# A hybrid attention block on one core: first loads in order of need, first low parts on GpSimd, and attention keys padded with zeros to 128 rows

## The chip, the core and the metric

The kernel runs on one core of one Trainium2 chip. The metric is the device time of one execution in microseconds (us); the number for the kernel before is the median of three runs. One more execution was taken by the hardware profiler, and every row shown here is from it.

Engine names: PE is TensorE (matrix multiply), PEld its weight loads, DVE is VectorE, ACT is ScalarE, POOL is GpSimd. SP only issues transfers. L394 is line 394 of the kernel.

## What is computed

One decoder layer, cut to what matters (512 tokens, width 1024, everything in float32):

```
h     = rms_norm(x, norm1_g)
proj  = h @ w_in                       # attention q, k, v; GLA q, k, v, r, low rank gate; branch gates
q, k  = rms_norm(q, gq), rms_norm(k, gk)      # 3 groups x 8 heads of 64
A     = softmax attention of 3 groups (window, dilation) = (128,1), (512,4), (2048,16),
        merged per head slot by the softmax denominators
B     = gated linear attention, 4 heads, rms_norm * silu(r)
x     = x + (sigmoid(gA) * (A @ w_attn) + sigmoid(gB) * (B @ w_gla)) @ w_out
x     = x + relu(rms_norm(x, norm2_g) @ w_up)^2 @ w_down
```

## The kernel before

**Products in three parts.** Every large matrix product is done with both operands split into a high part (type fp32r) and a low part: `split` (L105) makes a weight's high part `whi` by a copy on ACT (L78) and its low part `wlo = raw - whi` on DVE (L81), 128x1024 elements at a time. A product is then three matmuls of 128x512 for each 128x128 block: high with high, high with low, low with high (L155 to L157 in `mm_tok`, L136 to L138 in `mm_cols`). Below, such a matmul is called a projection matmul.

**Start.** x comes in four tiles of 128 tokens, 0.5 MB each; the first 512 columns of w_in in two loads of 1 MB (`raws`); norm1_g is broadcast to all 128 partitions by one 0.5 MB transfer, `g1b` (L203). The loads are issued from two queues: x0 and the weights from SP, `g1b` and the other x tiles from ACT (L202 to L208). For each tile `norm_in` squares x on ACT with a sum, `rsqrt` alternates DVE and ACT, L218 multiplies by the factor and by `g1b` on DVE; `trans_in` turns the tile on PE (8 transposes, L224), ACT copies the turned tile as high part `hTh`, DVE makes the low part `hTl`. Between two tiles stands one `split` of 2 of the 8 blocks of rows of the first weights. ACT and DVE keep the order in which this is written (`manual_schedule`, L232); PE's and POOL's order comes from the scheduler. POOL meanwhile makes the masks (affine selects at L262 to L288) and issues small column loads (L255, L96). Its order is fixed when the program is built, and no engine overtakes within its own order.

The first `mm_tok` uses the four splits of the start: 96 projection matmuls, over 4 token tiles and 8 row blocks. The second one follows; after 48 of its matmuls come the first turns of `qkv` (L328, 4 transposes each).

**Attention.** `qkv` (L307) makes for each group q and k, normalises them per head, and turns them so that a tile holds two heads on its 128 partitions: head 2p in rows 0 to 63, head 2p+1 in rows 64 to 127. The learned gains go in as a scale `gqk` when k is copied from PSUM to SBUF on ACT (L329). `attend` (L343) does for four tiles of 128 queries and for pairs of heads: scores on PE (L379 for the first group, L394 for the other two), masked row maximum on DVE (L357), exponential on ACT, four transposes of the probabilities on PE (L363), a copy on DVE (L365), product with v on PE (L369). A score matmul reads 64 rows of q and 64 rows of k: its array form is 64x128. Projection matmuls of the next products stand between these steps in PE's order. A float32 matmul that is not a transpose leaves two MATMUL records in the trace: 32 score matmuls at L379 are 64 records, 64 at L394 are 128.

PSUM has 5 banks for products (`mm`) and 3 for everything else (`aux`). Big SBUF tiles live in numbered slots that are used again.

Of the kernel before, what the change touches and what calls it, by code (L numbers as in the profile page):

```python
# [16 lines left out]
P = 128  # L17
# [24 lines left out]
def kernel(ctx: ExitStack, tc: tile.TileContext, x, norm1_g, w_in, q_g, k_g,  # L42
# [153 lines left out]
    g1b = slot(8, [P, D], "g1b")  # L196
    raws = [slot(10 + j, [P, 4, 512], f"raw{j}") for j in range(2)]

    def load_in(j):
        nc.sync.dma_start(raws[j], w_in[4 * j * P:4 * (j + 1) * P, 0:512].rearrange("(k p) n -> p k n", p=P))  # L200

    nc.sync.dma_start(xs[0][:, 0], x[0:P])  # L202
    nc.scalar.dma_start(g1b, bass.AP(tensor=norm1_g.tensor, offset=norm1_g.offset, ap=[[0, P], [1, D]]))  # L203
    load_in(0)
    nc.scalar.dma_start(xs[0][:, 1], x[P:2 * P])
    load_in(1)
    for i in (2, 3):
        nc.scalar.dma_start(xs[1][:, i - 2], x[i * P:(i + 1) * P])  # L208

    def norm_in(i):  # L210
        xi, hi_ = xs[i // 2][:, i % 2], hs[i // 2][:, i % 2]
        ss = sm(1, "ss")
        act(hi_, xi, AF.Square, accum_out=ss)
        r = sm(1, "r")
        rsqrt(r, ss, D, 1)
        for j in range(2):
            cs = slice(j * 512, (j + 1) * 512)
            nc.vector.scalar_tensor_tensor(hi_[:, cs], xi[:, cs], r, g1b[:, cs], op0=OP.mult, op1=OP.mult)  # L218

    def trans_in(i):  # L220
        bs = [aux() for _ in range(2)]
        hi_ = hs[i // 2][:, i % 2]
        for k in range(KB):
            nc.tensor.transpose(bs[k // 4][:, k % 4 * P:(k % 4 + 1) * P], hi_[:, k * P:(k + 1) * P], ident)  # L224
        for j in range(2):
            bv = bs[j].rearrange("p (k t) -> p k t", k=4)
            dh = hT.hi[j][:, :, i * P:(i + 1) * P]
            act(dh, bv, AF.Copy)
            last = tt(hT.lo[j][:, :, i * P:(i + 1) * P], bv, dh.bitcast(F32), OP.subtract)
        return last  # L230

    with tc.manual_schedule(engines={mybir.EngineType.Activation, mybir.EngineType.DVE}):  # L232
        def split_in():
            j = len(first)
            first.append(split(raws[j // 2][:, j % 2 * 2:j % 2 * 2 + 2], [2, 512]))

        norm_in(0)
# [7 lines left out]
        trans_in(2)  # L245
        norm_in(3)
        split_in()
        last = trans_in(3)


    with tc.issue_after(last.ins):
        qk_cols = consts.tile([P, 2], F32, name="qk_cols")
        for j, g in enumerate((q_g, k_g)):
            for hf in range(2):
# [3 lines left out]
                                       op0=OP.mult, op1=OP.mult)  # L258

# [47 lines left out]
    def qkv(g, lhs, sq, sk, sv):  # L307
        res = []
        for kind, s in ((0, sq), (1, sk)):
            banks = mm_tok(w_in, kind * 1536 + g * 512, lhs)  # L310
            dst = slot(s, [P, 4, S], f"a{kind}{g}")
            for i in range(NT):
# [12 lines left out]
                def turn(s2=s2, d=dst[:, :, i * P:(i + 1) * P], kw={"scale": gqk} if kind else {}):  # L325
# [6 lines left out]
            res.append(dst)  # L332
# [54 lines left out]
    q2T, k2T, v2 = qkv(1, hT.perm, 4, 5, 6)  # L387
    q3T, k3T, v3 = qkv(2, hT.perm, 7, 8, 13)
    o23 = slot(9, [P, NT, 512], "o23")

    def scores23(dst, pr, hf, i):
        r = slice(hf * E, hf * E + E)
# [505 lines left out]
```

## Time and profile before

| what | value |
|---|---|
| median of three runs | 1044.24 us (1043.93 to 1044.44) |
| the profiled execution's own time | 1045.75 us |
| its span, first to last instruction | 1043.8 us |
| PE busy | 1019.7 us, 98% of the span |
| DVE, ACT, POOL busy | 661.7, 501.6, 74.5 us |
| mean granted TensorE clock | 0.998 of full speed |

How to read it: the profiled execution took 1.5 us more than the median and its span leaves out some 2 us around the program. Busy time of matmuls overlaps, because the next one starts before the last has ended: for PE one reads the distance between starts, not the duration. In a row of the timeline the first number is the start, the second the time from the first start to the last end of the instructions merged in it, the number behind x their count, and in brackets stands the idle time before with what ended it.

### The profile page before, as it was taken

The numbers are of one execution on the slowest core, as the hardware profiler recorded it, in microseconds if no ns is written. First come the engines' busy times: TensorE is split into PE (matmuls) and PEld (weight loads), VectorE is DVE, ScalarE is ACT, GpSimd is POOL, SyncE is SP. The second block draws the span as 40 slices with busy tenths as digits, with TensorE's granted clock in tenths as the row PEclk, the third lists the DMA queues.
The fourth block names the chain that finished last, engine by engine and source line by source line (L and its number), as shares of the span: only waits on it lengthen the run. The fifth ranks groups of instructions, "written<-read, shape, count | busy, mean of one in ns | idle before, by whom it ended". The sixth has DMA issues, their size and how long they took to land.

```text
span 1043.8 us, 12458 instructions
## 1 busy us (share of the span) xinstructions
PE 1019.7 (98%) x4768; PEld 857.3 (82%) x4768; DVE 661.7 (63%) x1113; ACT 501.6 (48%) x835; POOL 74.5 (7%) x112
## 2 busy tenths in 40 slices
PE   4999999999999999999999999999999999999998
PEld 3888889999888788788888888877888888888886
DVE  4654354535444632889866747985885795796695
ACT  4434343424433423667645973365553553553552
POOL 9110001001000000010002200000000000000000
PEclk9999999999999999999999999999999999999999
DMA  7222102223201312312122234263133224225102
GB/s 262 72 91 81 41 1 81 81 89 101 94 1 41 93 61 81 121 41 81 41 82 76 86 130 162 72 206 114 43 123 120 80 82 160 82 81 161 41 1 80
DMA packets 63898, 92.36 MB, mean 88 GB/s; under 512 B 3232, under 2 KB 37024, under 8 KB 63840
## 3 DMA queue, kind: packets, MB, share of 16 engines
q1 hardware_dynamic: 61056, 86.02, 25.0%
q10 hardware_dynamic: 2368, 5.28, 1.4%
q8 instruction: 37, 0.61, 0.2%
q0 software_dynamic: 416, 0.28, 0.2%
q14 instruction: 21, 0.17, 0.0%
HBM read 89.44 MB, written 2.13 MB: 88 GB/s over the span
## 4 chain that ended last, share of the span: by engine, by line
PE 94%; DVE 3%; ACT 2%; DMA 1%; issue 0%; SPq 0%; DVEq 0%
PE mm L136 11%; PE mm L137 11%; PE mm L138 11%; PE mm L155 10%; PE mm L157 10%; PE mm L156 9%; PE mm L730 4%; PE mm L729 4%; PE mm L731 4%; PE aux L369 3%; PE aux L731 2%; PE aux L730 2%; PE aux L729 2%; PE aux L394 2%; PE aux L363 2%; PE aux L379 2%
## 5 line engine op out<-in xcount | busy, mean ns | idle before, releaser
L81 DVE TENSOR_TENSOR wlo<-wraw,whi 128x1024 fp32r<-128x1024 f32 x127 | 155.5, 1225 | 147.0 <-ACT whi L78 145.1
L78 ACT ACTIVATE whi<-wraw 128x1024 fp32r<-128x1024 f32 x127 | 134.3, 1057 | 186.1 <-PE mm L157 83.8
L155 PE MATMUL mm<-whi,hTh 128*128 128x512 f32 x416 | 171.4, 412 | 4.9 <-ACT hTh L78 4.8
L157 PE MATMUL mm<-whi,hTl 128*128 128x512 f32 x416 | 167.4, 403 | 0.0
L156 PE MATMUL mm<-wlo,hTh 128*128 128x512 f32 x416 | 166.4, 400 | 0.1
L155 PEld LDWEIGHTS mm<-whi,hTh 128*128 128x128 f32 x416 | 102.3, 246 | 15.6 <-ACT hTh L78 6.0
L156 PEld LDWEIGHTS mm<-wlo,hTh 128*128 128x128 f32 x416 | 102.4, 246 | 10.0 <-issue 1.0
L157 PEld LDWEIGHTS mm<-whi,hTl 128*128 128x128 f32 x416 | 101.9, 245 | 10.2 <-issue 1.0
L136 PE MATMUL mm<-xgh,whi 128*128 128x512 f32 x240 | 93.4, 389 | 0.0
L137 PE MATMUL mm<-xgl,whi 128*128 128x512 f32 x240 | 93.4, 389 | 0.0
L138 PE MATMUL mm<-xgh,wlo 128*128 128x512 f32 x240 | 93.4, 389 | 0.0
L729 PE MATMUL mm<-whi,left 128*128 128x512 f32 x200 | 78.0, 390 | 0.7 <-ACT whi L78 0.7
L730 PE MATMUL mm<-wlo,left 128*128 128x512 f32 x200 | 77.8, 390 | 0.5 <-DVE wlo L81 0.5
L136 PE MATMUL mm<-hTh,whi 128*128 128x512 f32 x192 | 77.6, 404 | 0.0
L731 PE MATMUL mm<-whi,left 128*128 128x512 f32 x200 | 77.2, 389 | 0.0
L138 PE MATMUL mm<-hTh,wlo 128*128 128x512 f32 x192 | 76.5, 398 | 0.0
L137 PE MATMUL mm<-hTl,whi 128*128 128x512 f32 x192 | 76.4, 398 | 0.0
L78 ACT ACTIVATE whi<-traw 128x1024 fp32r<-128x1024 f32 x40 | 42.4, 1059 | 46.0 <-PE mm L731 22.3
L365 DVE COPY pt<-aux 128x512 f32<-128x512 f32 (+1 forms) x32 | 21.1, 658 | 64.9 <-PE aux L363 64.7
L78 ACT ACTIVATE p<-p,nmx 128x256 f32<-128x256 f32 (+1 forms) x64 | 31.2, 488 | 59.9 <-DVE nmx L357 59.9
L81 DVE TENSOR_TENSOR left<-tmp,left 128x256 fp32r<-128x256 f32 (+1 forms) x40 | 43.2, 1088 | 22.8 <-ACT left L78 22.7
L138 PEld LDWEIGHTS mm<-xgh,wlo 128*128 128x128 f32 x240 | 45.0, 188 | 9.4
(241 smaller groups left out, 1868.3 us busy)
## 6 DMA issues: line engine op xcount, KB each, us to landing
wraw<-in_w_in_dram SPq DMA_DIRECT2D x36, 1024.0 KB, 5.1
wraw<-in_w_ff_up_dram SPq DMA_DIRECT2D x16, 1024.0 KB, 5.5
traw<-in_w_ff_down_dram SPq DMA_DIRECT2D x12, 1024.0 KB, 5.3
wraw<-in_w_gla_branch_dram SPq DMA_DIRECT2D x4, 1024.0 KB, 5.1
wraw<-in_w_ff_down_dram SPq DMA_DIRECT2D x4, 1024.0 KB, 5.1
traw<-in_w_out_dram SPq DMA_DIRECT2D x3, 1024.0 KB, 7.2
raw<-in_w_in_dram SPq DMA_DIRECT2D x2, 1024.0 KB, 14.2
wraw<-in_w_attn_branch_dram SPq DMA_DIRECT2D x2, 1024.0 KB, 5.1
```

The source lines that it names most:

```text
L78: nc.scalar.activation(o, i, f, **kw)
L81: return nc.vector.tensor_tensor(o, a, b, op)
L136: nc.tensor.matmul(b, hi[:, k], rh, start=(k == 0), stop=False)
L137: nc.tensor.matmul(b, hi[:, k], rl, start=False, stop=False)
L138: mm = nc.tensor.matmul(b, lo[:, k], rh, start=False, stop=(k == nk - 1))
L155: nc.tensor.matmul(banks[i], lh, hi[:, kk], start=(k == 0), stop=False)
L156: nc.tensor.matmul(banks[i], lh, lo[:, kk], start=False, stop=False)
L157: mm = nc.tensor.matmul(banks[i], ll, hi[:, kk], start=False, stop=(k == nk - 1))
L369: nc.tensor.matmul(ob[:, s * E:(s + 1) * E], pt[:, (m * nk + n) * P:(m * nk + n + 1) * P], values(n, s, i), start=(n == 0), stop=(n == nk ...
L729: nc.tensor.matmul(banks[i], lh, hi[:, jk], start=f, stop=False, skip_group_check=True)
L730: nc.tensor.matmul(banks[i], lh, lo[:, jk], start=False, stop=False, skip_group_check=True)
L731: nc.tensor.matmul(banks[i], ll, hi[:, jk], start=False, stop=l, skip_group_check=True)
```

## The change

1. All first loads are issued from SP in the order x0, w0, x1, w1, x2, w2, x3, w3, with w_in in four pieces of 0.5 MB. norm1_g comes as one row of 4 KB on ACT's queue and is spread over the partitions by two float32 matmuls with a row of ones (L216 of the new kernel); the result stays in one `mm` and one `aux` bank until the last tile is scaled. The order of the norm's steps on ACT and DVE is changed; the last two tiles share one `rsqrt`.
2. The low parts of the first four splits are made by POOL and not by DVE.
3. k is kept twice for each group, once for the even heads and once for the odd ones: both copies come from the same PSUM bank, scaled by a column `gqk2` that is zero on the other head's 64 rows. A score matmul then reads all 128 rows of q and k; the zeros take the other head out. It takes 12 more ACT copies and three more slots.

```diff
--- before.py
+++ after.py
@@ -108,7 +108,7 @@
         n_split[0] += 1
         with tc.high_priority() if n_split[0] > 4 else nullcontext():
             act(hi, raw_ap, AF.Copy)
-            tt(lo, raw_ap, hi.bitcast(F32), OP.subtract)
+            (nc.vector if n_split[0] > 4 else nc.gpsimd).tensor_tensor(lo, raw_ap, hi.bitcast(F32), OP.subtract)
         return hi, lo
...
@@ -193,59 +193,81 @@
-    g1b = slot(8, [P, D], "g1b")
     raws = [slot(10 + j, [P, 4, 512], f"raw{j}") for j in range(2)]
+    def load_x(i):
+        nc.sync.dma_start(xs[i // 2][:, i % 2], x[i * P:(i + 1) * P])
+
     def load_in(j):
-        nc.sync.dma_start(raws[j], w_in[4 * j * P:4 * (j + 1) * P, 0:512].rearrange("(k p) n -> p k n", p=P))
-
-    nc.sync.dma_start(xs[0][:, 0], x[0:P])
-    nc.scalar.dma_start(g1b, bass.AP(tensor=norm1_g.tensor, offset=norm1_g.offset, ap=[[0, P], [1, D]]))
-    load_in(0)
-    nc.scalar.dma_start(xs[0][:, 1], x[P:2 * P])
-    load_in(1)
-    for i in (2, 3):
-        nc.scalar.dma_start(xs[1][:, i - 2], x[i * P:(i + 1) * P])
...
+        nc.sync.dma_start(raws[j // 2][:, j % 2 * 2:j % 2 * 2 + 2],
+                          w_in[2 * j * P:2 * (j + 1) * P, 0:512].rearrange("(k p) n -> p k n", p=P))
+
+    g1r = slot(8, [P, D], "g1r")[0:1]
+    nc.scalar.dma_start(g1r, norm1_g)
+    for i in range(NT):
+        load_x(i)
+        load_in(i)
+
+    one_r = small.tile([1, P], F32, name="one_r", tag="one_r", bufs=1)
+    nc.vector.memset(one_r, 1.0)
+    g1b = [mm_bank(), aux()]
+    for j in range(2):
+        nc.tensor.matmul(g1b[j], one_r, g1r[:, j * 512:(j + 1) * 512], start=True, stop=True)
...
+        square_in(0)
+        rsqrt(r4[:, 0:1], ss4[:, 0:1], D, 1)
+        scale_in(0)
         split_in()
-        trans_in(0)
-        norm_in(1)
+        square_in(1)
+        rsqrt(r4[:, 1:2], ss4[:, 1:2], D, 1)
+        b0 = turn_in(0)
+        scale_in(1)
+        parts_in(0, b0)
         split_in()
-        trans_in(1)
-        norm_in(2)
+        square_in(2)
+        square_in(3)
+        rsqrt(r4[:, 2:4], ss4[:, 2:4], D, 2)
+        b1 = turn_in(1)
+        scale_in(2)
+        parts_in(1, b1)
         split_in()
...
+        gqk2 = consts.tile([P, 2], F32, name="gqk2")
+        nc.vector.memset(gqk2, 0.0)
+        for hf in range(2):
+            nc.vector.tensor_copy(gqk2[hf * E:(hf + 1) * E, hf:hf + 1], gqk[hf * E:(hf + 1) * E])
...
@@ -322,14 +351,16 @@
-                    act(d, b.rearrange("p (k t) -> p k t", k=4), AF.Copy, **kw)
+                    for n, d in enumerate(dst):
+                        act(d[:, :, i * P:(i + 1) * P], b.rearrange("p (k t) -> p k t", k=4), AF.Copy,
+                            **({"scale": gqk2[:, n:n + 1]} if kind else {}))
...
-    q1T, k1T, v1 = qkv(0, hT.nat, 9, 10, 11)
+    q1T, k1T, v1 = qkv(0, hT.nat, (9,), (10, 14), 11)
     o1 = slot(12, [P, NT, 512], "o1")

     def scores1(dst, pr, hf, i):
-        r = slice(hf * E, hf * E + E)
         lo = max(i - 1, 0) * P
-        nc.tensor.matmul(dst, q1T[r, pr, i * P:(i + 1) * P], k1T[r, pr, lo:(i + 1) * P], start=True, stop=True)
+        nc.tensor.matmul(dst, q1T[:, pr, i * P:(i + 1) * P], k1T[hf][:, pr, lo:(i + 1) * P], start=True, stop=True)
...
-    q2T, k2T, v2 = qkv(1, hT.perm, 4, 5, 6)
-    q3T, k3T, v3 = qkv(2, hT.perm, 7, 8, 13)
+    q2T, k2T, v2 = qkv(1, hT.perm, (4,), (5, 15), 6)
+    q3T, k3T, v3 = qkv(2, hT.perm, (7,), (8, 10), 13)
...
-            nc.tensor.matmul(dst[:, n * P:(n + 1) * P], q_[r, pr, i * P:(i + 1) * P],
-                             k_[r, pr, i * P:(i + 1) * P], start=True, stop=True)
+            nc.tensor.matmul(dst[:, n * P:(n + 1) * P], q_[:, pr, i * P:(i + 1) * P],
+                             k_[hf][:, pr, i * P:(i + 1) * P], start=True, stop=True)
```

Where instructions stand now. First the start of PE, before. Numbers behind tile names tell buffers apart: `whi_122` and `wlo_123` are the two parts of the first split, `whi_153` the high part of the second:

```order
L155 MATMUL mm_326<-whi_122,hTh0_89 128x512
L156 MATMUL mm_326<-wlo_123,hTh0_89 128x512
L157 MATMUL mm_326<-whi_122,hTl0_91 128x512
L155 MATMUL mm_326<-whi_153,hTh0_89 128x512
L224 MATMUL aux_157<-ident_82,h0_95 128x128 x4
L224 MATMUL aux_158<-ident_82,h0_95 128x128 x4
L155 MATMUL mm_327<-whi_122,hTh0_89 128x512
```

And the start of PE now, where the parts of the first split are `whi_130` and `wlo_131`, those of the second `whi_159` and `wlo_160`:

```order
L155 MATMUL mm_324<-whi_130,hTh0_89 128x512
L156 MATMUL mm_324<-wlo_131,hTh0_89 128x512
L157 MATMUL mm_324<-whi_130,hTl0_91 128x512
L155 MATMUL mm_324<-whi_159,hTh0_89 128x512
L156 MATMUL mm_324<-wlo_160,hTh0_89 128x512
L157 MATMUL mm_324<-whi_159,hTl0_91 128x512
L155 MATMUL mm_325<-whi_130,hTh0_89 128x512
```

The second split's low part is now asked for by PE after seven projection matmuls, ahead of the first product of the second token tile (bank mm_325). The first matmul that reads the third split's low part stands at the 50th place, the first that reads the fourth's at the 74th of the 96.

Second, POOL, around that low part. Before, at the end of the first mask:

```order
L286 AFFINE_SELECT f_259<-f_259 128x64
L96 DMA gbias_314<-in_gla_gate_bias_dram 128x4x1
L288 CAST pm1_258<-f_259 128x256
L284 AFFINE_SELECT f_271<-f_271 128x64 x3
L286 AFFINE_SELECT f_271<-f_271 128x64 x3
```

Now:

```order
L313 AFFINE_SELECT f_257<-f_257 128x64
L96 DMA gbias_312<-in_gla_gate_bias_dram 128x4x1
L111 TENSOR_TENSOR wlo_160<-raw0_97,whi_159 128x1024
L315 CAST pm1_256<-f_257 128x256
L311 AFFINE_SELECT f_269<-f_269 128x64 x3
L313 AFFINE_SELECT f_269<-f_269 128x64 x3
```

The four low parts stand in POOL's order among the masks: the first behind the identity (all but one of the small loads and all masks come after it), the second here, the third (`wlo_190`) in the middle of the last mask, behind its first four selects, the fourth behind all masks and column loads.

Third, PE in the attention over groups 2 and 3, now; in the order of before the same rows stand in the same order, with L394 for the scores and L363 for the transposes:

```order
L394 MATMUL aux<-ident,p_2273 128x128 x2
L423 MATMUL aux<-a_2026,a_1817 128x128
L423 MATMUL aux<-a_1478,a_1269 128x128
L423 MATMUL aux<-a_2026,a_1817 128x128
L137 MATMUL mm<-hTl_92,whi 128x512
L400 MATMUL aux<-v_1692,pt 128x64
```

Here L423 are the scores, L394 the transposes of the probabilities and L400 the products with v. No instruction of PE moved in either attention: there are 43 unbroken runs of score matmuls in both kernels, 21 in the first group and 22 in the other two.

## Rows read from the trace of the kernel before

**Rows 1.** Windows: stretch, length, busy PE, PEld, DVE, ACT, POOL (instructions), granted clock, DMA share, GB/s.

```profile
92.00:158.00 66.00, 66.00 (x337) 54.49 (x336) 29.45 (x93) 26.83 (x83) 2.08 (x2) 1.00 0.10 32
278.00:345.00 67.00, 66.97 (x422) 53.85 (x421) 28.14 (x86) 27.74 (x80) 0.61 (x1) 1.00 0.11 33
```

**Rows 2.** Timeline of PE in the attention over groups 2 and 3.

```profile
285.26 0.38 PE L363 MATMUL aux<-ident,p 128*128 128x128 f32 x2
285.56 0.48 PE L394 MATMUL aux<-a,a 64*128 64x128 f32 x2
285.98 0.44 PE L363 MATMUL aux<-ident,p 128*128 128x128 f32 x2
286.35 0.93 PE L394 MATMUL aux<-a,a 64*128 64x128 f32 x6
287.21 0.50 PE L137 MATMUL mm<-hTl,whi 128*128 128x512 f32 x1
287.55 1.00 PE L369 MATMUL aux<-v,pt 128*128 128x64 f32 x8
288.48 1.16 PE L394 MATMUL aux<-a,a 64*128 64x128 f32 x8
289.57 0.66 PE L363 MATMUL aux<-ident,p 128*128 128x128 f32 x4
289.98 0.48 PE L138 MATMUL mm<-hTh,wlo 128*128 128x512 f32 x1
```

**Rows 3.** Timeline of PE, 256-column matmuls: scores of the first group.

```profile
102.86 0.70 PE L379 MATMUL aux<-a,a 64*128 64x256 f32 x2
103.49 0.33 PE L363 MATMUL aux<-ident,p 128*128 128x128 f32 x1
```

**Rows 4.** Timeline of PE, 256-column matmuls over 128 rows, in the gated linear attention.

```profile
487.54 1.02 PE L596 MATMUL aux<-vg,kt 128*128 128x256 f32 x4
488.40 1.03 PE L606 MATMUL aux<-vg,pps 128*128 128x256 f32 x4
```

**Rows 5.** Timeline of PE, around the first turns of q.

```profile
55.31 0.40 PE L157 MATMUL mm<-whi,hTl 128*128 128x512 f32 x1
55.54 0.60 PE L328 MATMUL aux<-ident,s 128*128 128x128 f32 x4
```

**Rows 6.** Timeline of PE, the first scores of groups 2 and 3.

```profile
278.40 1.26 PE L394 MATMUL aux<-a,a 64*128 64x128 f32 x16
```

**Rows 7.** Timeline of ACT, end of the last exponential before the transposes at 289.57.

```profile
288.80 0.19 ACT L78 ACTIVATION_READ_ACCUMULATOR p<-p,nmx 128x1 f32 x1
```

**Rows 8.** Timeline of POOL, start: first and last of the rows behind the identity, and two between.

```profile
2.42 0.58 POOL L255 DMA_DIRECT2D qk_cols<-in_attn_q_norm_g_dram  x1
...
5.44 1.87 POOL L284 TENSOR_SCALAR_AFFINE_SELECT f<-f 128x64 f32<-128x64 f32 x3
...
12.25 0.64 POOL L284 TENSOR_SCALAR_AFFINE_SELECT f<-f 128x64 f32<-128x64 f32 x3
...
27.45 0.50 POOL L288 CAST qm<-f 128x384 uint8<-128x384 f32 x1
```

**Rows 9.** Groups of POOL: shapes, count, then busy us, mean ns, idle before.

```profile
L317 POOL TENSOR_TENSOR s<-rw 128x512 f32<-128x512 f32 x24 | 24.8, 1042 | 217.3 <-ACT rw L78 132.2 <-PE aux L328 69.0 <-ACT ry L78 9.4
L650 POOL TENSOR_TENSOR rs<-rs,e 128x512 f32<-128x512 f32 x8 | 11.7, 1476 | 44.0 <-ACT e L78 41.5 <-issue 2.5
```

**Rows 10.** Timeline of ACT, start.

```profile
5.86 1.06 ACT L78 ACTIVATE h<-x 128x1024 f32<-128x1024 f32 x1 [3.77 <-DMA x<-in_x_dram]
...
7.46 0.20 ACT L78 ACTIVATE ry<-ry 128x1 f32<-128x1 f32 x1
14.19 1.06 ACT L78 ACTIVATE whi<-raw 128x1024 fp32r<-128x1024 f32 x1 [6.52 <-DMA raw<-in_w_in_dram]
```

**Rows 11.** Timeline of PE, its first projection matmul.

```profile
15.78 0.80 PE L155 MATMUL mm<-whi,hTh 128*128 128x512 f32 x1 [4.60 <-ACT hTh L78]
```

**Rows 12.** Windows, as in rows 1, while the first tile of x comes in.

```profile
2.00:6.00 4.00, 0.00 (x0) 0.00 (x0) 0.00 (x0) 0.23 (x2) 3.91 (x12) 1.00 0.94 294
```

More of the change, by code (lines that the diff above doesn't have):

```diff
@@ L204 @@
-    load_in(0)
-    nc.scalar.dma_start(xs[0][:, 1], x[P:2 * P])
-    load_in(1)
-    for i in (2, 3):
-        nc.scalar.dma_start(xs[1][:, i - 2], x[i * P:(i + 1) * P])
[L210 to L215, printed above, removed]
+        nc.sync.dma_start(raws[j // 2][:, j % 2 * 2:j % 2 * 2 + 2],
+                          w_in[2 * j * P:2 * (j + 1) * P, 0:512].rearrange("(k p) n -> p k n", p=P))
@@ new lines, with square_in @@
+    g1r = slot(8, [P, D], "g1r")[0:1]
[8 more added lines that the diff above has]
+        nc.tensor.matmul(g1b[j], one_r, g1r[:, j * 512:(j + 1) * 512], start=True, stop=True)
+    ss4 = consts.tile([P, 4], F32, name="ss4")
+    r4 = consts.tile([P, 4], F32, name="r4")
+    def square_in(i):
+        act(hs[i // 2][:, i % 2], xs[i // 2][:, i % 2], AF.Square, accum_out=ss4[:, i:i + 1])
@@ L216, in norm_in, with scale_in, turn_in @@
+    def scale_in(i):
         for j in range(2):
             cs = slice(j * 512, (j + 1) * 512)
-            nc.vector.scalar_tensor_tensor(hi_[:, cs], xi[:, cs], r, g1b[:, cs], op0=OP.mult, op1=OP.mult)
-    def trans_in(i):
+            nc.vector.scalar_tensor_tensor(hs[i // 2][:, i % 2, cs], xs[i // 2][:, i % 2, cs], r4[:, i:i + 1],
+                                           g1b[j], op0=OP.mult, op1=OP.mult)
+    def turn_in(i):
         bs = [aux() for _ in range(2)]
-        hi_ = hs[i // 2][:, i % 2]
@@ L223, in trans_in, with parts_in @@
         for k in range(KB):
-            nc.tensor.transpose(bs[k // 4][:, k % 4 * P:(k % 4 + 1) * P], hi_[:, k * P:(k + 1) * P], ident)
+            nc.tensor.transpose(bs[k // 4][:, k % 4 * P:(k % 4 + 1) * P], hs[i // 2][:, i % 2, k * P:(k + 1) * P],
+                                ident)
+        return [b.rearrange("p (k t) -> p k t", k=4) for b in bs]
+    def parts_in(i, bs):
         for j in range(2):
-            bv = bs[j].rearrange("p (k t) -> p k t", k=4)
             dh = hT.hi[j][:, :, i * P:(i + 1) * P]
-            act(dh, bv, AF.Copy)
@@ L229, in trans_in, with split_in @@
-            last = tt(hT.lo[j][:, :, i * P:(i + 1) * P], bv, dh.bitcast(F32), OP.subtract)
-        return last
+            act(dh, bs[j], AF.Copy)
+            last = tt(hT.lo[j][:, :, i * P:(i + 1) * P], bs[j], dh.bitcast(F32), OP.subtract)
+        return last
+    def split_in():
+        j = len(first)
+        first.append(split(raws[j // 2][:, j % 2 * 2:j % 2 * 2 + 2], [2, 512]))
     with tc.manual_schedule(engines={mybir.EngineType.Activation, mybir.EngineType.DVE}):
-        def split_in():
-            j = len(first)
-            first.append(split(raws[j // 2][:, j % 2 * 2:j % 2 * 2 + 2], [2, 512]))
@@ L237 @@
-        norm_in(0)
+        square_in(0)
+        rsqrt(r4[:, 0:1], ss4[:, 0:1], D, 1)
+        scale_in(0)
         split_in()
-        trans_in(0)
-        norm_in(1)
-        split_in()
-        trans_in(1)
-        norm_in(2)
+        square_in(1)
[3 more added lines that the diff above has]
+        parts_in(0, b0)
+        split_in()
+        square_in(2)
+        square_in(3)
+        rsqrt(r4[:, 2:4], ss4[:, 2:4], D, 2)
+        b1 = turn_in(1)
@@ L244 @@
+        scale_in(2)
+        parts_in(1, b1)
         split_in()
-        trans_in(2)
-        norm_in(3)
+        b2 = turn_in(2)
+        scale_in(3)
+        parts_in(2, b2)
         split_in()
-        last = trans_in(3)
+        last = parts_in(3, turn_in(3))
     with tc.issue_after(last.ins):
@@ L308, in qkv @@
         res = []
-        for kind, s in ((0, sq), (1, sk)):
+        for kind, ss_ in ((0, sq), (1, sk)):
             banks = mm_tok(w_in, kind * 1536 + g * 512, lhs)
-            dst = slot(s, [P, 4, S], f"a{kind}{g}")
+            dst = [slot(s, [P, 4, S], f"a{kind}{g}{n}") for n, s in enumerate(ss_)]
             for i in range(NT):
@@ L323, in qkv, with turn @@
                    r[:, :, None].to_broadcast([P, NH, E]), OP.mult)
-                def turn(s2=s2, d=dst[:, :, i * P:(i + 1) * P], kw={"scale": gqk} if kind else {}):
+                def turn(s2=s2, dst=dst, i=i, kind=kind):
                     b = aux()
@@ L328, in turn @@
                         nc.tensor.transpose(b[:, k * P:(k + 1) * P], s2[:, k * P:(k + 1) * P], ident)
-                    act(d, b.rearrange("p (k t) -> p k t", k=4), AF.Copy, **kw)
+                    for n, d in enumerate(dst):
+                        act(d[:, :, i * P:(i + 1) * P], b.rearrange("p (k t) -> p k t", k=4), AF.Copy,
+                            **({"scale": gqk2[:, n:n + 1]} if kind else {}))
                 later.append(turn)
-            res.append(dst)
+            res.append(dst if kind else dst[0])
         banks = mm_tok(w_in, 3072 + g * 512, lhs)
```

1 line of the change is left out of this document (removed).

## The prediction

> **What bounds the kernel now.** I read the windows first, for the two attentions: PE is busy 66.00 of 66 us and 66.97 of 67, ACT and DVE under 30 [rows 1]. So what shortens PE's own stream there shortens the program, and what it adds lengthens it. Then the timeline of PE inside such a stretch [rows 2], by the distance between starts. A projection matmul takes 0.23 us (55.31 to 55.54) [rows 5]. Last the start, where PE has nothing to read: its first projection matmul starts at 15.78 [rows 11], because ACT waits until 14.19 for w_in [rows 10], behind x and the broadcast row. The same engine orders with other durations give the new time, so I take the change in these two places.
>
> **The scores.** What does one run of 64-row scores cost beyond its records? A run of 8 lasts 1.09 us (288.48 to 289.57), a run of 2 lasts 0.42 (285.56 to 285.98) [rows 2]: six records more are 0.67 us, 0.112 each, and 0.19 is left over in either run. The run of 6 agrees: 0.86 less 0.67. There is more at the edges. Two transposes ahead of scores take 0.30 (285.26 to 285.56) where they need 0.22: 0.09 at the entry. The four transposes behind scores last 0.66 [rows 2], four behind a projection matmul 0.60 [rows 5]: 0.06 at the first instruction after. Together 0.34 us per run. With 256 columns it is the same: two records take 0.63 (102.86 to 103.49) [rows 3], while 128-row float32 matmuls of 256 columns follow each other every 0.215 (four from 487.54 to 488.40), and two kinds of them (L596, then L606) follow without a pause [rows 4]; 0.63 less 0.43 is 0.20.
>
> The reading that I choose: the array changes its form from 128 to 64 rows and back, and the weights of the next instruction aren't loaded ahead across such a change. With 128 rows everywhere it goes. A record itself stays as long: 0.112 and 0.215 are what 128-row matmuls show too.
>
> There is a loss as well. Where an even and an odd head follow each other directly, two 64-row records run at once: the first 16 records of the second attention last 1.26 us, hardly more than 8 others (1.16) [rows 6, 2]. Such pairs stand only in the two runs in which both banks are free, 4 pairs there and 8 here. They lose 12 times 0.112, 1.3 us, and keep 2 times 0.34 of gain. The Trainium skill, TensorEngine Tiling (Array Packing), Key Properties, says that row tiles work in parallel; were every score record paired, the loss would be half of all score records. The trace shows 12 pairs, and the rule is at work in no other run.
>
> Sum for the scores: 41 times 0.34 is 13.9, less 0.6 for the two paired runs: **13.3 us less**. Does another wait take its place? The transposes at 289.57 have had their data since 288.99 [rows 7]; PE will come 0.4 earlier there, with exit, entry and restart gone, and still finds them ready. I take nothing off. From below, the stalls might not belong to the form at all (gain nothing, loss 1.3). From above, runs that end at a projection matmul might gain a little more, 0.05 each for 16 of them: 14 us.
>
> The 12 added ACT copies (128x512; one of 128x1024 takes 1.06 [rows 10], so some 0.6 to 0.7 us each, an estimate) are hidden: ACT is busy 27 to 28 us of 66 [rows 1]. They hold an `aux` bank that much longer; turns stand 12 projection matmuls (2.8 us) apart. If that cover were gone, 8 us on ACT would still not be on PE's path. The slots taken again (14, 15, 10, 8) are next written well after the last read: kT, vg and the GLA pairs come behind the second attention.
>
> **The start.** First what it wins. x0 is 0.52 MB, and in the time that it comes in now 294 GB/s arrive [rows 12]; alone in front, from about 2.0 us, that is 1.8 us and some 0.3 to the signal, so ACT squares x0 at 4.1 and not at 5.86 [rows 10]. ACT's second small step of the norm ends 1.80 us after the square's start (7.66 less 5.86) [rows 10], here 5.9; the first weights, 0.52 MB behind x0, are there at 5.9 too. The first high part takes 1.06 [rows 10] and ends at 7.0. Transposes and first projection matmul follow at about 10, against 15.78 [rows 11]. The two float32 matmuls that spread norm1_g run while PE has nothing else; if the 4 KB row came late, the first tile's scaling would wait for it. The banks they hold leave two `aux` banks for turning: a wait inside the wait below.
>
> Now the price. POOL makes the four low parts, in its fixed order among masks and column loads. That other work takes from 2.42 to 27.95, **25.5 us** [rows 8], today off everybody's path. In the new order all of it but the identity stands behind the first low part and in front of the fourth. Nothing on PE reads the masks until the attention, but PE reads the low parts. One low part on POOL isn't in the trace. The nearest rows are two-input operations on 128x512: 1.04 us with the same tile twice, 1.48 mean with two tiles and DVE beside them [rows 9]; for 128x1024 that is 2.1 to 3.0, and I take 2.6. The Trainium skill, GPSIMD Engine Reference, Elementwise, has 4497 ns for 2048 columns, against 2293 on VectorE; half of it, 2.25, is a page's estimate that would make the sum below 1.4 us smaller.
>
> So the first low part stands from 7.0 to 9.6; the second behind the rows up to about 11.9, done at 21.7; the fourth at 7.0 + 4 x 2.6 + 25.5 = **42.9**. PE meets the second as its eighth projection matmul and then stands still from about 14 to 21.7. The third comes some 4 to 5 us of masks and one low part before the fourth, at about 36; PE needs it at its 50th matmul, 42 of them and 16 transposes after 21.7, about 34. The fourth is read by the 74th of 96: 23 remain, 5.3 us, and 48 of the next product up to the first turns, 11.0 us. Those turns then start at 59.2, against 55.54 [rows 5]: **3.7 us more**. PE's own work is the floor: should POOL be quicker, the 89 projection matmuls that follow the second low part (20.5 us), 16 transposes and the restart after a wait bind from then on, which leaves the start about where it is now, at best 1 us earlier.
>
> **Sum.** 1045.75 (the profiled execution) - 13.3 + 3.7 = 1036.2. The median lies 1.5 below the profiled execution, so I predict **1034.6**.
>
> **The rivals.**
> Half of the scores' gain stays away. Of the 86 ends of score runs 51 touch a transpose; if a transpose next to a 128-row float32 matmul keeps a stall of 0.09, 4.6 us are kept: 1039; if the whole 0.17 per end, 1043. For it: no row shows that neighbourhood with 128 rows. Against it: a projection matmul next to a transpose costs nothing, 0.23 up to its start [rows 5]. Chance 0.12.
>
> POOL is quicker than its rows. The affine selects take 0.61 each at 5.44 and 0.20 at 12.25 [rows 8]; at the quick pace all through, the fourth low part is no longer last and PE's own work binds: 3.7 becomes -1, the time 1030. Against it: the same column loads are issued in the same places, and the slow selects stand behind them. Chance 0.13.
>
> **Slower: the stalls are not the array's form.** A float32 instruction whose data come late also shows a late weight load. If the 0.34 come from such waits for banks and not from 64 rows, 128 rows keep them; the pairs cost 1.3 and the start 3.7: 1034.6 + 13.3 + 1.3 = 1049. It decides from 0.24 of the 0.34 us kept per run. For it: the entry looks like a late load. Against it: all three runs of rows 2 leave the same 0.19, whatever stands before, and a wait would differ. Chance 0.09.
>
> **How the numbers follow.** The forecast's own case has 0.66: 1032 to 1037.5, with 2.1 and 3.0 for a low part. For 8 in 10 I go down to the quick POOL with a little more gain on the exits, 1029, and up to the lower half of the first rival, 1041. A difference of 0.2%, 2 us, is about what a measurement of this kernel can tell. Faster by more than that: forecast, quick POOL and nearly all of the half gain, 0.88; within it: the rest of the half gain, 0.03; slower: 0.09.
>
> **What would show it.** Right: in the timeline of PE, 8 score records from start to next start in about 0.90 us and 2 in 0.22, with form 128*128; PE's share of idle before the second attention only at the start; on POOL the fourth low part near 43, and the first turns near 59. Wrong: score runs still 0.19 over their records; PE waiting for DVE or ACT inside attention; first turns before 56 or after 61; an `aux` bank that makes PE wait for ACT's second copy of k.

## The result, and the profile after

The change takes **1033.74 us** (median of 4 runs, 1031.74 to 1034.02) where the kernel before takes 1044.34 in the same comparison: a ratio of **0.9891, 95% interval 0.9878 to 0.9904**. The profiled execution took 1034.02 us, its span is 1032.31; that of before took 1045.75 with 1043.84. Its span is 11.5 us shorter, and four landmarks on PE tell where:

| landmark, us from the start | before | after | difference | added here |
|---|---|---|---|---|
| first turns of q, group 1 | 55.54 | 56.99 | +1.45 | +1.45 |
| first scores of group 1 | 92.22 | 93.61 | +1.39 | -0.06 |
| first scores of groups 2 and 3 | 278.40 | 272.99 | -5.41 | **-6.80** |
| turns of the outputs of groups 2 and 3 | 355.12 | 343.72 | -11.40 | **-5.99** |
| end of the span | 1043.84 | 1032.31 | -11.53 | -0.13 |

The start lost 1.45 us, the two attentions won 12.79, the 689 us behind them did not move. First the timeline of PE after, in the attention of groups 2 and 3, the counterpart of [rows 2] (start us, busy us, engine, line, operation, tiles, rows*columns of the array, shape, count):

```profile
280.05 0.38 PE L394 MATMUL aux<-ident,p 128*128 128x128 f32 x2
280.27 0.39 PE L423 MATMUL aux<-a,a 128*128 128x128 f32 x2
280.49 0.38 PE L394 MATMUL aux<-ident,p 128*128 128x128 f32 x2
280.71 0.83 PE L423 MATMUL aux<-a,a 128*128 128x128 f32 x6
281.30 0.47 PE L137 MATMUL mm<-hTl,whi 128*128 128x512 f32 x1
281.66 1.10 PE L400 MATMUL aux<-v,pt 128*128 128x64 f32 x8
282.60 1.11 PE L423 MATMUL aux<-a,a 128*128 128x128 f32 x8
283.54 0.60 PE L394 MATMUL aux<-ident,p 128*128 128x128 f32 x4
```

Read from start to start: two scores 0.22 (0.42 before), six 0.59 (0.86), eight 0.94 (1.09); two transposes ahead of scores 0.22 (0.30). The projection matmul behind the six starts early and its own distance is 0.36 instead of 0.23, so the two are best read together: 0.95, where six records and one such matmul need 0.90. The busy times say little here, since records of a pipelined engine overlap. The 256-column scores of group 1, the counterpart of [rows 3], take 0.43 for two, against 0.63:

```profile
103.67 0.60 PE L409 MATMUL aux<-a,a 128*128 128x256 f32 x2
104.10 0.27 PE L394 MATMUL aux<-ident,p 128*128 128x128 f32 x1
```

Then the start. POOL's four low parts with the last of the mask work, and PE around its wait for the second one (in brackets the idle time ahead and what ended it):

```profile
7.27 2.36 POOL L111 TENSOR_TENSOR wlo<-raw,whi 128x1024 fp32r<-128x1024 f32 x1 [4.77 <-ACT whi L78]
18.55 2.36 POOL L111 TENSOR_TENSOR wlo<-raw,whi 128x1024 fp32r<-128x1024 f32 x1
30.91 2.38 POOL L111 TENSOR_TENSOR wlo<-raw,whi 128x1024 fp32r<-128x1024 f32 x1
36.20 0.50 POOL L315 CAST qm<-f 128x384 uint8<-128x384 f32 x1
36.67 2.39 POOL L111 TENSOR_TENSOR wlo<-raw,whi 128x1024 fp32r<-128x1024 f32 x1
```

```profile
11.30 0.79 PE L155 MATMUL mm<-whi,hTh 128*128 128x512 f32 x1 [1.54 <-ACT hTh L78]
16.77 0.40 PE L155 MATMUL mm<-whi,hTh 128*128 128x512 f32 x1
20.96 0.80 PE L156 MATMUL mm<-wlo,hTh 128*128 128x512 f32 x1 [3.79 <-POOL wlo L111]
21.55 0.63 PE L157 MATMUL mm<-whi,hTl 128*128 128x512 f32 x1
21.98 0.63 PE L155 MATMUL mm<-whi,hTh 128*128 128x512 f32 x1
26.98 0.40 PE L156 MATMUL mm<-wlo,hTh 128*128 128x512 f32 x1
27.22 0.39 PE L155 MATMUL mm<-whi,hTh 128*128 128x512 f32 x1
56.99 0.60 PE L357 MATMUL aux<-ident,s 128*128 128x128 f32 x4
```

PE's first projection matmul stands 4.48 us earlier than in [rows 11], and all of that and 1.45 more is lost again before 57 us. One wait of 3.79 us is in the row at 20.96. The second loss has no bracket: from 21.55 on the matmuls start 0.43 us apart, and only from 26.98 on 0.24.

### The profile page after: what moved, and what is told of

The parts are those of the page before. It is cut to its first block, busy times and chain, and to the rows that moved or that the text cites. A ratio compares the mean times of both kernels' runs of the same rounds, so it can differ in the third digit from the quotient of the medians.

```text
span 1032.3 us, 12479 instructions
## 1 busy us (share of the span) xinstructions
PE 1012.2 (98%) x4772; PEld 860.3 (83%) x4772; DVE 665.7 (64%) x1109; ACT 507.3 (49%) x845; POOL 81.8 (8%) x116
## 4 chain that ended last, share of the span: by engine, by line
PE 92%; DVE 4%; ACT 1%; POOL 1%; issue 1%; DMA 0%; SPq 0%; POOLq 0%; DVEq 0%
PE mm L136 11%; PE mm L137 10%; PE mm L138 10%; PE mm L155 10%; PE mm L157 9%; PE mm L156 9%; PE mm L759 4%; PE mm L758 4%; PE mm L760 4%; PE aux L400 3%; PE aux L759 2%; PE aux L760 2%; PE aux L758 2%; PE aux L423 1%; PE aux L394 1%; PE aux L409 1%
## 5 line engine op out<-in xcount | busy, mean ns | idle before, releaser
L155 PEld LDWEIGHTS mm<-whi,hTh 128*128 128x128 f32 x416 | 102.8, 247 | 10.8 <-ACT hTh L78 2.3
L78 ACT ACTIVATE whi<-traw 128x1024 fp32r<-128x1024 f32 x40 | 42.3, 1058 | 46.1 <-PE mm L760 22.3
L136 PEld LDWEIGHTS mm<-xgh,whi 128*128 128x128 f32 x240 | 45.0, 188 | 9.4
```

The costliest lines, as they stand in the source:

```text
L136: nc.tensor.matmul(b, hi[:, k], rh, start=(k == 0), stop=False)
L155: nc.tensor.matmul(banks[i], lh, hi[:, kk], start=(k == 0), stop=False)
```

## The experiments

Two theories were open. **Scores**: the gain is of the array's form (64 rows or 128), or of something that the padding also changed (a tile per head, more copies, other slots, banks that come free at another time). **Start**: the loss is GpSimd's slow subtraction, its place in GpSimd's queue, or something else. All runs, each with the kernel before beside it (1044.34 us beside the change, 1044.55 beside the four runs that follow it in the table, 1044.45 and 1044.32 beside the two with the masks late that take 1026.72 and 1025.66, 1044.12 beside the other three):

| run | us | ratio to before, 95% | first turns | first scores of group 1 to those of groups 2 and 3 |
|---|---|---|---|---|
| the change | 1033.74 | 0.9878 to 0.9904 | 56.99 | 179.38 |
| start alone | 1045.70 | 1.0000 to 1.0018 | 57.17 | 186.75 |
| scores alone | 1032.60 | 0.9869 to 0.9896 | 55.96 | 179.26 |
| padded keys, 64 rows read | 1045.19 | 0.9997 to 1.0015 | 56.49 | 186.17 |
| low parts on VectorE | 1027.82 | 0.9822 to 0.9849 | 51.65 | 179.24 |
| masks late, first try | 1032.12 | 0.9870 to 0.9897 | 56.36 | 179.24 |
| masks late, put right | 1026.72 | 0.9818 to 0.9845 | 51.15 | 179.38 |
| VectorE, row spread by DMA | 1028.33 | 0.9834 to 0.9860 | 51.30 | 179.28 |
| VectorE, TensorE busy ahead | 1026.03 | 0.9812 to 0.9839 | 50.71 | 179.26 |
| masks late and busy ahead | **1025.66** | 0.9808 to 0.9835 | 49.52 | 179.36 |

**Each half alone.** The start's edits alone are put onto the kernel before:

> The kernel before with the start's edits alone (order of loads, norm's row spread by TensorE, first four low parts on GpSimd); keys and scores as before. My theory: the two halves of the change are independent, the start costs what the first turns lost between the two traces (55.54 to 56.99 us, +1.45), so about 1045.7 us (1045 to 1046.5), with the first turns near 57.0 and the interval from the first score of group 1 to that of groups 2 and 3 as before, 186.2 us. Rival one: the start's loss is made up later, 1044.0 to 1044.6. Rival two: part of the gain after the first scores comes from the start (other order of loads for the weights that follow), then the interval is under 185 us here and the time under 1043.

Then the edits on keys and scores alone:

> The kernel before with the padded keys and the scores over 128 rows alone; the start as before. My theory: the two intervals shrink as in the change (186.18 to 179.4 and 76.72 to 70.7 us), so 1044.3 - 12.8 = 1031.5 us (1031 to 1032.2), faster than the change by 1.45 to 2.3 us. Rival: the start's edits are needed for a part of it, then 1033 or more.

Measured 1045.70 and 1032.60: 1.15 us lost and 11.95 won beside the 1044.55 of their comparison, together 10.8 against 10.6 for the change. The halves are independent within the scatter; the interval between the scores goes with the score edits alone (186.75 and 179.26; that the first is 0.57 above the 186.18 of before stays open). The second run missed its range (1031 to 1032.2) by 0.4, and the last section has a cause for 1.4 us and more of such scatter.

**Form, or something else.** The edit, in both score functions:

```
-        nc.tensor.matmul(dst, q1T[:, pr, i * P:(i + 1) * P], k1T[hf][:, pr, lo:(i + 1) * P], start=True, stop=True)
+        r = slice(hf * E, hf * E + E)
+        nc.tensor.matmul(dst, q1T[r, pr, i * P:(i + 1) * P], k1T[hf][r, pr, lo:(i + 1) * P], start=True, stop=True)
```

> The change with one thing undone: keys still kept per head with zeros, with all twelve additional copies, but the score matmuls read the 64 rows of their head alone, so that their shape is 64 rows again. Data, copies, banks, order and loads are those of the change. My theory (the array's change between 128 and 64 rows holds up the loading of weights): the stalls come back at every run of scores, 41 x 0.34 = 13.9 us at most, 12.8 by what the intervals lost: 1046.5 us (1045 to 1048), first instructions after a score run 0.2 us and more apart again, start to start. Rival (the stalls were of the two heads' shared key tile, of slots or of banks, and padding took them away by other means): 1033.7, within 2 us.

Measured 1045.19, all of the gain gone. PE's timeline, group 1 and then groups 2 and 3, with keys per head as in the change:

```profile
103.87 0.70 PE L410 MATMUL aux<-a,a 64*128 64x256 f32 x2
104.49 0.33 PE L394 MATMUL aux<-ident,p 128*128 128x128 f32 x1
...
286.25 0.38 PE L394 MATMUL aux<-ident,p 128*128 128x128 f32 x2
286.56 0.48 PE L424 MATMUL aux<-a,a 64*128 64x128 f32 x2
286.97 0.44 PE L394 MATMUL aux<-ident,p 128*128 128x128 f32 x2
287.34 0.93 PE L424 MATMUL aux<-a,a 64*128 64x128 f32 x6
288.20 0.50 PE L137 MATMUL mm<-hTl,whi 128*128 128x512 f32 x1
```

Two scores are at 0.41 and 0.62 again, six at 0.86, the transposes ahead at 0.31, and the interval is 186.17 against 186.18 before. Copies, slots, banks and the order on PE are those of the change, so the stall is of the form. The run also prices the twelve additional copies: beside the start alone (1045.70) it is not slower, so they cost nothing that can be measured.

How the stall comes about can be read from PEld, the weight loads, in front of a run of two scores. First before, then now:

```profile
285.56 0.29 PEld L394 LDWEIGHTS aux<-a,a 64*128 64x128 f32 x2 [0.17 <-issue]
```

```profile
280.16 0.30 PEld L423 LDWEIGHTS aux<-a,a 128*128 128x128 f32 x2
```

Before, the loading for the first score starts together with its matmul (285.56 in [rows 2]), behind 0.17 us in which PEld stood and nothing in the profile held it. Now it starts at 280.16, while the last transpose runs, 0.11 ahead of its matmul (280.27). With 64 rows read from the padded keys it starts with the matmul again (286.55 and 286.56). The Trainium skill, TensorEngine Tiling (Array Packing), Key Properties, says that changing the tiling mode drains TensorE, and gives no price. The trace agrees that the change of form costs time, and 12.79 us over 43 runs of scores are on average 0.30 us for each way there and back.

**Low parts on VectorE.** One line:

```
-            (nc.vector if n_split[0] > 4 else nc.gpsimd).tensor_tensor(lo, raw_ap, hi.bitcast(F32), OP.subtract)
+            tt(lo, raw_ap, hi.bitcast(F32), OP.subtract)
```

> The change with its first four low parts on VectorE again, all else kept. My theory: TensorE stands from 16.8 to 20.96 us for the second low part that GpSimd delivers behind its masks; on VectorE (1.25 us each) it is there before, so the first projection closes up by most of that 3.8 us, and the first turns come 2 to 4 us earlier: 1030 to 1032 us. Rival: VectorE's 5 us of additional work delay the scaling of the rows (x g1b) that the transposes wait for, and give it back: 1033 to 1035.

Measured 1027.82, 2.2 us below the range: the first turns come 5.34 us earlier, more than the wait of 3.79. The matmul that waited at 20.96, the eighth of the projection, now starts 3.58 us earlier:

```profile
17.38 0.63 PE L156 MATMUL mm<-wlo,hTh 128*128 128x512 f32 x1
```

From it to the first turns pass 34.27 us instead of 36.03. Most of these 1.76 us are the clock. Windows from 16 to 21 and from 21 to 26 us (length, busy us and instructions of PE, PEld, DVE, ACT, POOL, granted clock, DMA share, GB/s), first of the change:

```profile
16.00:21.00 5.00, 1.21 (x5) 0.60 (x3) 4.46 (x3) 2.33 (x5) 4.98 (x7) 0.90 0.73 266
21.00:26.00 5.00, 5.00 (x14) 3.97 (x15) 4.35 (x8) 0.36 (x1) 5.00 (x18) 0.50 0.04 2
```

and with the low parts on VectorE:

```profile
16.00:21.00 5.00, 5.00 (x20) 3.93 (x20) 4.90 (x10) 2.15 (x4) 5.00 (x13) 1.00 0.74 281
21.00:26.00 5.00, 4.96 (x26) 3.80 (x25) 4.26 (x7) 2.89 (x5) 5.00 (x13) 1.00 0.05 2
```

TensorE stood from 17.17 to 20.96, and the stretch after it has a granted clock of 0.50, the lower level, 1.2 GHz; without the standing it is 1.00, 2.4 GHz. Both rows of 21 to 26 call PE fully busy, with 14 instructions in the one and 26 in the other. From 20.96 to 26.53 the change ran nine projection matmuls and eight transposes in 5.6 us that take some 3.1 at the later spacing (0.23 and 0.13 each): some 2.5 us, which no wait list shows. The run with VectorE's low parts pays 0.8 of its own behind 17.38: four of its matmuls still start 0.43 apart, up to 19.08, although the window of 16 to 21 prints 1.00 (the last section says why). So the standing cost the change both its length and the slow stretch behind it.

**GpSimd's speed, or its place?** The low parts stay on GpSimd, and the masks go behind them. In this first try the four small column loads of gate, output norm, branch and second norm went elsewhere too, and with them `nbb_col`, a VectorE operation on one of these columns (these lines stand behind the dots):

```
+    with tc.issue_after(last.ins), tc.issue_after(lows[3].ins):
         mask_a = consts.tile([P, 256], F32, name="mask_a")
...
-        pair_mask = {m: block_mask(f"pm{m}", 256, [(64 * i, 64 // m, m, 2 * m, 0, m) for i in range(NT)])
-                     for m in (1, 32)}
...
     o1 = slot(12, [P, NT, 512], "o1")
...
+    pair_mask = {m: block_mask(f"pm{m}", 256, [(64 * i, 64 // m, m, 2 * m, 0, m) for i in range(NT)])
+                 for m in (1, 32)}
```

> The change with its first four low parts still on GpSimd, but with no mask between them there: the two attention masks are issued behind the fourth low part, the pair and quad masks and their selects behind the squares of group 1. Asks whether the 5.9 us that VectorE's low parts won lay in GpSimd's slower subtraction (2.36 against 1.24 us) or in its place behind the masks. Theory one, the place: the second low part can start when its high part is there, near 14 us, and ends near 16.4, before TensorE wants it at 16.8; TensorE does not stand, its granted clock stays at 1.0 between 20 and 25 us, first turns at 51.5 to 53 us, and the time is 1027.5 to 1029.5. Theory two, the engine: VectorE's small operations of the row norms are held while GpSimd subtracts (2.6 us each beside the second low part), the scaling of rows 2 and 3 stays late, first turns at 54 to 57 us and 1030.5 to 1034. A risk of its own: the late masks fall beside the attention of group 1, and hold VectorE there; the interval from its first score to that of groups 2 and 3 would then be above 179.4.

Measured 1032.12, with first turns at 56.36. Both lie in theory two's ranges, but not for its reason: the edit had made a wait of its own. Two of PE's waits (us in total, times, longest), then the operation on VectorE that caused the longest:

```profile
PE mm L156 <- ACT hTh L78: 4.5, 2, 3.1
PE mm L157 <- POOL wlo L112: 0.2, 1, 0.2
```

```profile
19.70 0.17 DVE L407 TENSOR_SCALAR nbb_col<-bb_col 128x16 f32<-128x16 f32 x1 [5.87 <-DMA bb_col<-in_branch_gate_bias_dram]
19.79 0.16 DVE L185 TENSOR_SCALAR rv<-ss 128x2 f32<-128x2 f32 x1
```

Nothing at the start reads nbb_col, but it stood ahead of the roots of rows 2 and 3 in VectorE's order, and the roots came 0.09 us behind it. ScalarE's next step waited for them until 19.98, and ScalarE's high part of rows 1, next in its order, came at 20.33. PE's wait for GpSimd had already shrunk from 3.79 to 0.2. TensorE stood 3.08 us for the new reason, and the granted clock was 0.50 again from 20 to 25. Put right, with nbb_col behind the start and the column loads behind the fourth low part:

> The run before with masks late, put right: there the columns' loads had slipped ahead of the second low part on GpSimd (11.10 to 14.68 us), and VectorE's nbb_col, queued ahead of the roots of rows 2 and 3, waited 5.87 us for its column, so that TensorE stood 3.08 us for rows 1 for a reason of its own. Now the column loads come behind the fourth low part and nbb_col behind the start. Theory one (GpSimd's place behind the masks was the cost): the second low part runs from about 12.5 to 14.9 us, TensorE does not stand between 16 and 21 us, granted clock 1.0 from 20 to 25, first turns at 51.5 to 53 us and the time 1027.5 to 1029.5, as with VectorE's low parts. Theory two (the engine): VectorE's 128x2 root operations at 15.2 us are held while GpSimd subtracts, or TensorE waits for the third low part (2.4 us each from 20 us on): first turns at 54 us or later, 1030.5 us or more.

Measured 1026.72, with first turns at 51.15: theory one, and 0.8 and 0.35 us better than its ranges. GpSimd's low parts:

```profile
6.97 2.36 POOL L112 TENSOR_TENSOR wlo<-raw,whi 128x1024 fp32r<-128x1024 f32 x1 [4.47 <-ACT whi L78]
12.57 2.37 POOL L112 TENSOR_TENSOR wlo<-raw,whi 128x1024 fp32r<-128x1024 f32 x1 [1.71 <-DMA raw<-in_w_in_dram]
17.65 2.40 POOL L112 TENSOR_TENSOR wlo<-raw,whi 128x1024 fp32r<-128x1024 f32 x1 [2.71 <-ACT whi L78]
22.46 2.40 POOL L112 TENSOR_TENSOR wlo<-raw,whi 128x1024 fp32r<-128x1024 f32 x1 [2.41 <-ACT whi L78]
```

As slow as before, each is now ready when TensorE comes: no wait for GpSimd is left in PE's list, and the time is not above that with VectorE. The place was the cost, not the engine. The masks, now beside group 1's attention, leave the interval at 179.38.

The place had a second effect that the wait list hides. In the change a root on VectorE lasted until 17.78, beside masks on GpSimd (last section), and ScalarE waited for it:

```profile
17.82 0.20 ACT L78 ACTIVATE ry<-rv 128x2 f32<-128x2 f32 x1 [2.64 <-DVE rv L184]
```

So its high part of rows 1, which TensorE reads two matmuls after the second low part, came at 18.16; with the masks late it came at 15.56, with VectorE's low parts at 15.79. Had the second low part been there in time, TensorE would have met this wait next. Both runs take away the two together; how much each is worth alone is not shown.

**The spreading of norm's row.** The change's matmuls against the broadcast DMA, in the new order of loads, with low parts on VectorE:

> The change with low parts on VectorE (1027.8 us) and, beside it, norm's row spread over the partitions by one DMA of 512 KB on ScalarE's queue, as before, in place of the two matmuls; the new order of loads stays. Theory: the 512 KB go ahead of or beside the first rows of x, at the 294 to 300 GB/s of that stretch 1.7 us, so the first square, the first high part and the first projection matmul (11.3 us) come 1 to 1.7 us later, and so does the end: 1028.8 to 1029.5. Rival: the first projection waits for something else (the chain square, root, scaling, turns of rows 0, high part), the DMA lies beside it, and the time stays within 0.5 us of 1027.8.

Measured 1028.33, below the theory's range and 0.03 above the rival's. Each was half right. The first projection matmul does wait, longer than the theory said: it comes at 14.33 instead of 11.34. But the first turns are at 51.30, none later than the 51.65 without the DMA; the projection's matmuls start 0.23 apart from 16.98 on, where the run without it gets there at 19.08. The three microseconds that TensorE's spreading wins at its first matmul don't reach the first turns. The half microsecond between the two times is less than what the dip of the last section does, which this run's profiled execution has and the other's hasn't.

**TensorE busy ahead.** 6 transposes before and 8 behind the turns of rows 0, into a bank that is overwritten:

```
+    busy(ident, 6)
...
         b0 = turn_in(0)
+        busy(hs[0][:, 0, 0:P], 8)
```

> The change with low parts on VectorE (1027.8 us), and TensorE kept busy in its gaps before the first projection matmul: 6 additional transposes of the identity behind the spreading matmuls, 8 of a piece of the first rows behind their turns, into a bank that the projection overwrites later. In the run without them, the projection's matmuls from 11.3 to 18.7 us start 427 ns apart, and 213 to 230 from there on. Theory: that is the clock's lower level after standing, and with TensorE busy ahead the higher level comes earlier; 13 matmuls of 512 columns at 0.21 us less are 2.7 us at most, and with the waits for rows 1 between them 0.5 to 2.5 us remain: 1025.3 to 1027.3. Rival one: the high and low parts and the rows that arrive then bind, not the matmuls: within 0.4 us of 1027.8. Rival two: the level does not depend on it, and the 8 transposes push the first matmul back by up to 0.5 us: 1028 to 1028.5.

Measured 1026.03. The same projection matmuls without the transposes ahead, then with them:

```profile
16.10 0.63 PE L156 MATMUL mm<-wlo,hTh 128*128 128x512 f32 x1
16.52 0.63 PE L157 MATMUL mm<-whi,hTl 128*128 128x512 f32 x1
```

```profile
15.16 0.40 PE L158 MATMUL mm<-wlo,hTh 128*128 128x512 f32 x1
15.40 0.40 PE L159 MATMUL mm<-whi,hTl 128*128 128x512 f32 x1
```

From 0.42 to 0.24 between starts: work without a use, ahead of the first projection matmul, brought the higher level earlier. The first turns come 0.94 earlier, and the spans of the two profiled executions differ by 0.83 (1025.36 and 1024.53). The medians differ by 1.8, but the run without the transposes took 1027.07 and 1027.31 in two executions and 1028.33 and 1028.45 in the other two, and the intervals of the two ratios overlap: what the times show beyond the start is scatter, as far as is known. Last, both gains together:

> The run with late masks put right (1026.7 us, low parts on GpSimd) together with the 14 additional transposes that keep TensorE busy ahead of the first projection (they won 1.8 us on the version with VectorE's low parts). Theory: the two gains are of different stretches in part (the one ends TensorE's standing at 16.8 us, the other raises its clock before 16 us) and the matmuls from 13 to 18 us then start 230 ns apart: first turns at 49.8 to 50.7 us, time 1025 to 1026. Rival: with the matmuls quicker, the second or third low part of GpSimd (ending at 14.9 and 20.05 us) is late, and TensorE waits for it: 1026.3 to 1027.5.

Measured **1025.66**, 18.7 us below the kernel before of its comparison and the lowest median of all. The first turns, at 49.52, are 1.63 us ahead of masks late alone and 0.3 ahead of the range expected; the intervals of the two ratios overlap, so that step is shown by the trace and not by the times.

## Why the prediction was right

The prediction was 1034.6 us, the result 1033.74, within the range of the forecast's own case. Its two terms fared differently: the scores came out by the mechanism that was forecast, the start did not.

*Scores.* -13.3 predicted, -12.79 measured in the two intervals, and the mechanism stands: with the shape alone put back, the stalls are back and both intervals with them, and the rows of PEld show the reading that was chosen, weights not loaded ahead across the change. The excess inside a run, 0.19 before, is none now for two scores (0.22) and 0.04 for eight (0.94 where 0.90 were predicted); with 0.09 at the entry and 0.06 behind, a run of two gives back the 0.34 of the sum, a run of eight 0.29 or 0.30. That is where the term was a little too large. What the prediction called a loss is there as well: the first 16 scores of groups 2 and 3 take 1.70 us, against 1.19 in the run with padded keys and 64 rows. The half-gain rival is out, since a transpose beside a 128-row matmul keeps no stall (0.22 for two). So is the one for slower, which said that the stalls were waits: in the run with padded keys and 64 rows, data and banks were those of the change, and the stalls were there. The additional copies cost nothing, as predicted.

*Start.* +3.7 predicted, +1.45 measured, and that it came out a loss at all is partly luck: two errors of opposite sign. **The step that failed is "the fourth at 7.0 + 4 x 2.6 + 25.5 = 42.9", and with it that the fourth low part sets the first turns.** A low part took 2.36 to 2.39, not 2.6, and the mask and column work 22.3 us (39.06, the end of the fourth, less 7.27 and 9.49 for four parts), not 25.5. So it ended at 39.06, and TensorE waited neither for it nor for the third. What binds is PE's own work, as in the rival of the quick POOL. That rival said 1030 by "PE's own work is the floor", and it isn't 1030 because that floor was too low. From 20.96 on, the text's own count, 89 projection matmuls with 48 more up to the turns at 0.23, and 16 transposes at 0.13, is 33.6 us, which would bring the turns at 54.55, 1 us earlier than before; the trace has 36.03 (56.99 less 20.96). The 2.4 us between are the half clock after the standing. The prediction names a "restart after a wait" there and gives it no number.

The early landmarks were near: the square of x0 at 4.43 (predicted 4.1; no row shows the 0.3 us "to the signal" in that sum), the first high part's end at 7.18 (7.0), the second low part's at 20.91 (21.7). The first projection matmul came at 11.30, not at about 10, and TensorE stood from 17.17, not from about 14: the first matmuls started 0.43 apart and not 0.23, and PE stood 0.92 us among them ahead of the turning of rows 1.

Luck is in the sum, too. Between the profiled executions -9.6 us were predicted and -11.73 measured (1045.75 to 1034.02). The 1.5 us that were taken off for the median came out as 0.28, and that hides more than half of the miss of 2.1. The range, 1032 to 1037.5, is wider than the source that it names: 2.1 and 3.0 us for a low part give 1032.6 to 1036.2.

## What to carry to other kernels

A matmul over half of the array's rows, mixed with matmuls over all of them, pays at every change, here some 0.3 us for a run of two scores and for a run of eight; zeros in the unused rows cost nothing beside that, except where two half-array matmuls ran at once (0.5 us in one run of 16). When an operation is moved to a less busy engine, ask what stands ahead of it in that engine's order, not only how long it takes: on GpSimd, against VectorE, the same subtractions cost 5.3 us up to the first turns behind the masks and nothing ahead of them. And when TensorE stands for some microseconds, count what the clock takes after the wait as well, by the distance between starts: here 2.4 us behind a wait of 3.79.

## What was not expected of the hardware

*VectorE held beside GpSimd.* In the change, VectorE's small root operations on rows 2 and 3 took 2.57 and 2.67 us, one on a single column 2.93, and a low part of its own 3.34:

```profile
15.21 2.57 DVE L184 TENSOR_SCALAR rv<-ss 128x2 f32<-128x2 f32 x1 [1.22 <-ACT h L78]
18.29 2.67 DVE L188 SCALAR_TENSOR_TENSOR rv<-ry,rv 128x2 f32<-128x2 f32 x1 [0.51 <-ACT ry L78]
30.38 2.93 DVE L279 SCALAR_TENSOR_TENSOR gqk<-qk_cols 128x1 f32<-128x1 f32 x1
36.81 3.34 DVE L111 TENSOR_TENSOR wlo<-wraw,whi 128x1024 fp32r<-128x1024 f32 x1 [0.98 <-ACT whi L78]
```

The second ends at 20.96 and the third at 33.31, when low parts of GpSimd end (20.91 and 33.29); the fourth ends at 40.15, 1.09 us after the end of another (39.06), and takes 1.23 alone. In the run with late masks put right, where GpSimd does nothing then, the first root operation, at 15.01, takes 0.17. Operations that read a PSUM bank were not held: the scaling of rows 0 takes 0.74 beside the first low part. GpSimd can be the one that is held: with the low parts on VectorE, a select at 14.03 took 1.22 us beside VectorE's low part (13.93 to 15.15), one of the same shape ahead of it 0.23. The Trainium skill, SBUF — State Buffer, SBUF: two separate sides, says that GpSimd and VectorE share a pair of ports as an exclusive lock, for a whole instruction, when VectorE reads two inputs there or runs in a fast mode. The trace agrees on the three that end with or behind a subtraction, though two of them had started 0.26 and 0.53 us ahead of it (18.55 and 30.91); the one at 15.21 outlasted several of GpSimd's selects (14.43 to 17.75). Why these got no turn earlier stays open.

*A clock that dips in some executions only.* Near 700 us PE waits 1.4 us for xgh, with the dip and without it. Windows there, of the kernel before and then of the start alone:

```profile
708.00:711.00 3.00, 2.01 (x10) 1.37 (x11) 2.88 (x8) 2.50 (x6) 0.00 (x0) 0.93 0.46 130
711.00:714.00 3.00, 3.00 (x14) 2.64 (x13) 1.65 (x3) 1.48 (x3) 0.00 (x0) 0.50 0.62 220
```

```profile
710.00:713.00 3.00, 1.71 (x9) 1.15 (x10) 2.90 (x8) 2.50 (x6) 0.00 (x0) 1.00 0.39 98
713.00:716.00 3.00, 3.00 (x22) 2.52 (x21) 2.69 (x5) 2.60 (x5) 0.00 (x0) 1.00 0.73 253
```

The same work, with 14 matmuls in three microseconds in the one and 22 in the other. Of the eleven profiled executions four have the dip: before, the change, the scores alone and the row spread by DMA. From the end of that wait they take 334.8 to 335.6 us to the end of the span, the seven others 333.4. Why the clock dips in some and not in others is not shown. Differences of one microsecond between single executions therefore need a landmark ahead of the dip.

*A granted clock that isn't in the spacing.* From 11.3 to 16.5 us the change's projection matmuls that follow each other start 0.42 to 0.59 apart although the windows of that stretch print 1.00, as they do later with 0.23. The trace has no entry of the clock so early, and ahead of the first one the view prints 1.00. The first entry begins at 16.58 us in the change, 21.10 in the kernel before, 19.08 with low parts on VectorE, 12.56 with TensorE busy ahead and 25.32 with the start alone, each with the higher level, and from about there on the matmuls start 0.23 apart. In the first microseconds the distance between starts is the better witness.
